# Seven Strassen pairs for the merge gates, with operand sums made from a stored modulated x

## The chip, the core and the metric

The kernel runs on one core of a Trainium2 chip. Its engines work from queues of their own and wait for each other by semaphores: TensorE (PE in the profile; its weight loads are shown as PEld), VectorE (DVE), ScalarE (ACT) and GpSimd (POOL). SyncE (SP) issues nearly all loads; POOL issues the stores that the code calls `store`. The metric is the device time of one execution in microseconds. Three runs of the kernel before took 1413.15, 1414.62 and 1421.28 us; the median is 1414.62 us.

## The reference

One layer over 1024 tokens of width 1024, in two halves. The change is in the first, the token mixer:

```
h     = rmsnorm(x, pre_mix_g) * (1 + sc1) + sh1      # sc1, sh1: per channel, from c @ ada_w
proj  = h @ w_in                                     # GLU input, q k v, and the gates
u     = silu(layernorm(conv31(glu(proj))))           # causal depthwise convolution, 512 channels
y_conv = u @ w_conv_out
y_att  = stick_breaking_attention(q, k, v) @ w_att_out
merged = sigmoid(g_conv) * y_conv + sigmoid(g_att) * y_att
y      = merged @ w_o
```

The gates `g_conv` and `g_att` are 2048 columns of `h @ w_in`, each a sum over the 1024 channels of h. After this half come its residual with a norm, and a SwiGLU block of the same manner. All is float32.

## The kernel before

**Data.** Channels lie on the partitions and tokens along the free axis. h is held as eight tiles of 128 channels by 1024 tokens, each as two parts, `hhi[k]` and `hlo[k]`, whose sum is h: a product of two such numbers is made by three matmuls (high x high, high x low, low x high) into a float32 bank of PSUM. A matmul takes 128x128 weights and streams 512 tokens. The 16 tiles of h live in the pool `hp`, tag `act`, which has 16 buffers.

**Start.** For each k, DVE multiplies x by the norm's factor and the scale (`x_op`, L310; the result stays in the tile `xs[k]`), ACT adds the shift and rounds (`hi_op`, L313), and DVE makes the low part (`lo_op`, L316).

**Attention stage.** Four heads' pairs are worked off with a raised priority; projections for the next pair, the GLU and the convolution (`conv`, L461) stand between them. The convolution's output goes to DRAM, `u_d`.

**Gates.** The 2048 gate columns are 16 blocks of 128, and two neighbouring blocks make a pair i = 0 to 7. A plain gate block (list `PLAIN`, L611 on; tile `pg`) takes 8 x 3 x 2 = 48 matmuls. A Strassen pair takes the 2x2 block product (two output blocks by two halves of the channels, times two halves of the channels by two halves of the tokens) in seven block products of 4 x 3 = 12 matmuls each instead of eight. `B11`, `B21` and `B22` are quarters of h itself, read from `hhi` and `hlo`; `T1` to `T4` are differences and sums of quarters, each held as a high and a low part for j = 0 to 3. `NPL = 2` makes pairs 6 and 7 plain and pairs 0 to 5 Strassen pairs.

The six Strassen pairs are made in two steps. The *early products* (loop over `GPAIRS`, the last in the attention stage's block; tiles `k1`, `k2`, `ee`) are the two that need no T: A11 B11, which goes to DRAM as `e_d0`, and A12 B21, which added to it gives the first gate quarter. Then, in a new scope with a new pool `pg` in the place of the attention's pools, DVE rebuilds h in `f` (L664, L665: `hhi + hlo`), makes four sums (L667 to L670) and ACT and DVE split them (`make_t`); `other_five(i)` makes the other five products for each pair and the gates' sigmoids, with `e_d0` loaded back as `p1`. Gates go to DRAM as `s_d`.

**LN and merge.** `ln_all` loads `u_d` into `cr` tiles and does the layer norm and silu of the convolution. It stands after pair 0 (`LN_AT = 0`) with a slightly raised priority, and its tiles come from `hp`, tag `act`. `y_conv` (tile `pyc`) multiplies it by `w_conv_out` and the gates, `y_att` (the loop that follows, tile `pya`) does it for the attention; then come the output projection (`pwo`) and the SwiGLU block (from L958 on).

**Order.** A planner orders each engine's instructions: it follows a model of the engines and takes at each point the ready instruction that stands first in the code, priorities aside. A tile needs a free buffer of its tag; the pools that matter here are `wp` (`wraw`, `whi` and `wlo`: three buffers each, for weights as loaded and for their parts), `hp`, and in `pg` the tags `f` (2), `x` (7), `s` (4) and `op` (16). PSUM banks are `psm` (3) and `psg` (4 and one for LN), dealt out by `bkg`. The order is fixed when the program is built; semaphores hold it on the chip.

Of the kernel before, what the change touches and what calls it, by code (L numbers as in the profile page):

```python
# [18 lines left out]
P = 128  # L19
D = 1024  # L20
T = 1024
KT = D // P
CH = 512
# [14 lines left out]
SH_DVE = (5, 6, 7)  # L38
NADA = 5
LATER = 100000  # L40
NPL = 2
GORDER = (0, 1, 2, 3, 4, 5, 6, 7)
NXT = 7
NWT = 4
# [31 lines left out]
def tile_block(ctx: ExitStack, tc: tile.TileContext, xT, vecs, ada1, ada2, win, wv, wcv, wat, wo, w1, w2, cvw, out):  # L76
    nc = tc.nc
    act, dve, pool, pe = nc.scalar, nc.vector, nc.gpsimd, nc.tensor
# [12 lines left out]
    u_d = [dp.tile([NG, P, TM], F32, name=f"u_d{k}") for k in range(CONVT)]  # L91
    cb_d = dp.tile([P, D], F32, name="cb_d")
    s_d = [dp.tile([P, T], F32, name=f"s_d{n}") for n in range(2 * KT)]
    e_d0 = [dp.tile([P, CH], F32, name=f"e_d0_{i}") for i in range(KT)]
    g_d = [dp.tile([P, 2, 2, CH], F32, name=f"g_d{k}") for k in range(FH)]
    w_d = [dp.tile([P, 4, 2, CH], F32, name=f"w_d{k}") for k in range(FH)]

# [5 lines left out]
    def load(dst, src):  # L103
        return nc.sync.dma_start(dst, src)

    def store(dst, src):
        nc.gpsimd.dma_start(dst, src)
# [19 lines left out]
    mod = small.tile([P, 48], F32, name="mod")  # L127
# [68 lines left out]
    hhi, hlo = [], []  # L196
# [6 lines left out]
    def bank(name):  # L203
        return psm.tile([P, CH], F32, tag="main", name=name)
# [5 lines left out]
    sgp = mkpool(sS, "sgp")  # L210
    with ExitStack() as s0:
# [7 lines left out]
        aws, xs, w0s, w0raw = {}, [], [], []  # L219
# [12 lines left out]
        with tc.high_priority(offset=3 * SOONER):  # L232
# [4 lines left out]
            for k in range(KT):  # L237
                load_ada(k)
                if k in W0_AT:
                    raw = wp.tile([P, T], F32, tag="wraw", name=f"w0raw{len(w0raw)}")  # L240
# [74 lines left out]
        def lo_op(k):  # L315
            dve.scalar_tensor_tensor(hlo[k], xs[k], shift_of(k), hhi[k], op0=ALU.add, op1=ALU.subtract)  # L316
# [41 lines left out]
        for k in range(KT):  # L358
            kn = k + 1
            if kn < KT:  # L360
                if kn not in SH_DVE:
                    shift_act(kn)
                if kn + 1 < KT and kn + 1 not in SH_DVE:
                    shift_pe(kn + 1)
                x_op(kn)
                if kn <= 2:
                    w0_hi(kn)
                hi_op(kn)
                if kn + 1 < KT:
                    dots(kn + 1)  # L370
                if kn <= 2:
                    w0_lo(kn)
            if k:
                lo_op(k)
            ws = (q0b, k0b, gg0b)
            if k <= 1:
                for i in range(k + 1):
                    gemm_k(ws[i], w0s[i], k)
                for kk in range(k + 1):
                    gemm_k(ws[k + 1], w0s[k + 1], kk)  # L380
            else:
                for b_, w_ in zip(ws, w0s):
                    gemm_k(b_, w_, k)
# [3 lines left out]
        for c in range(NCH):  # L387
            sg = sgp.tile([P, CH], F32, tag="sg", name=f"sg0_{c}", bufs=2)
# [4 lines left out]
    HK = KT // 2  # L393
    GP = dve
    GPAIRS = GORDER[:KT - NPL]
# [3 lines left out]
    def w_op(name, src, hi_eng, lo_eng):  # L399
        t = wp.tile([P, 2, CH], F32R, tag=("whi", "wlo")[next(uid) % 2], name=name)  # L400
        copy_to(hi_eng, t[:, 0], src)
        lo_eng.tensor_tensor(t[:, 1], src, t[:, 0], op=ALU.subtract)
        return t[:, 0], t[:, 1]

    def prod0(bank_, w, b, first=True):
        for j in range(HK):
            cols = slice(j * P, (j + 1) * P)
            if b[0] == "T":
                mvs = B0[b, j][:, 0], B0[b, j][:, 1]
            else:  # L410
                k = j + (HK if b in ("B21", "B22") else 0)
                cs = slice(CH, T) if b == "B22" else slice(0, CH)
                mvs = hhi[k][:, cs], hlo[k][:, cs]
            for s, (st, mv) in enumerate(((0, 0), (0, 1), (1, 0))):
                pe.matmul(bank_, w[st][:, cols], mvs[mv], start=(first and j == 0 and s == 0),
                          stop=(j == HK - 1 and s == 2), skip_group_check=not first)

    with ExitStack() as sC:
        pc = mkpool(sC, "pc")
        with ExitStack() as sA:  # L420
# [181 lines left out]
            v = v_half(0)  # L602
# [8 lines left out]
            for n in PLAIN:  # L611
                gb = banks2(f"pg{n}")
                gemm(gb, load_w(win[20 + n], f"wg{n}"), h, range(KT))
                for c in range(NCH):
                    sg = sgp.tile([P, CH], F32, tag="sg", name=f"sg{n}_{c}", bufs=2)
                    act.activation(sg, gb[c], AF.Sigmoid, bias=0.0, scale=1.0)
                    store(s_d[n][:, c * CH:(c + 1) * CH], sg)
            for i in GPAIRS:
                raw = wp.tile([P, T], F32, tag="wraw", name=f"ew{i}")
                load(raw, win[20 + 2 * i])  # L620
                e = [sgp.tile([P, CH], F32, tag="sg", name=f"ee{q}_{i}", bufs=2) for q in range(2)]
                k1 = bank(f"k1_{i}")
                prod0(k1, w_op(f"a11_{i}", raw[:, :CH], act, dve), "B11")
                act.activation(e[0], k1, AF.Copy)
                store(e_d0[i], e[0])
                k2 = bank(f"k2_{i}")
                prod0(k2, w_op(f"a12_{i}", raw[:, CH:], act, dve), "B21")
                dve.tensor_tensor(e[1], k2, e[0], op=ALU.add)
                act.activation(e[1], e[1], AF.Sigmoid, bias=0.0, scale=1.0)
                store(s_d[2 * i][:, :CH], e[1])  # L630

    sV.close()
    with ExitStack() as sG:
# [6 lines left out]
        def xt(name):  # L640
            return pg.tile([P, CH], F32, tag="x", name=name, bufs=NXT)
# [6 lines left out]
        def bkg(name):  # L648
            if next(uidg) % 7 in (1, 4, 6):
                return bank(name)  # L650
            return psg.tile([P, CH], F32, tag="m", name=name)
# [4 lines left out]
        def make_t(name, src, hi_eng, lo_eng):  # L656
# [2 lines left out]
            lo_eng.tensor_tensor(t[:, 1], src, t[:, 0], op=ALU.subtract)  # L659
            return t  # L660

        for j in range(HK):
            f = [pg.tile([P, T], F32, tag="f", name=f"f{q}_{j}", bufs=2) for q in range(2)]
            dve.tensor_tensor(f[0], hhi[j], hlo[j], op=ALU.add)  # L664
            dve.tensor_tensor(f[1], hhi[HK + j], hlo[HK + j], op=ALU.add)  # L665
            b11, b12, b21, b22 = f[0][:, :CH], f[0][:, CH:], f[1][:, :CH], f[1][:, CH:]
            dve.tensor_tensor(b11, b12, b11, op=ALU.subtract)  # L667
            dve.tensor_tensor(b12, b22, b12, op=ALU.subtract)
            dve.tensor_tensor(b22, b22, b11, op=ALU.subtract)
            dve.tensor_tensor(b21, b21, b22, op=ALU.subtract)  # L670
            for b, src in (("T2", b22), ("T3", b12), ("T1", b11), ("T4", b21)):
                B0[b, j] = make_t(f"{b}o_{j}", src, act, dve)

        pairs, p1s = {}, {}

        def pair_load(i):
            wg = wp.tile([P, T], F32, tag="wraw", name=f"gw{i}a")
            load(wg, win[20 + 2 * i])
            wu = wp.tile([P, T], F32, tag="wraw", name=f"gw{i}b")
            load(wu, win[21 + 2 * i])  # L680
            pairs[i] = wg, wu
            p1s[i] = xt(f"ga{i}")
            load(p1s[i], e_d0[i])

        def sig_out(t, n, c):
            act.activation(t, t, AF.Sigmoid, bias=0.0, scale=1.0)
            store(s_d[n][:, c * CH:(c + 1) * CH], t)

        def other_five(i):
            wg, wu = pairs[i]  # L690
            p1 = p1s[i]
            a11, a12, a21, a22 = wg[:, :CH], wg[:, CH:], wu[:, :CH], wu[:, CH:]
            s1, s2, s3 = (st(f"g{nm}_{i}") for nm in ("s1", "s2", "s3"))
            v, w_, c21 = xt(f"gv_{i}"), xt(f"gw_{i}"), xt(f"gc_{i}")
            dve.tensor_tensor(s1, a21, a22, op=ALU.add)
            dve.tensor_tensor(s2, s1, a11, op=ALU.subtract)
            s2o = w_op(f"s2o_{i}", s2, act, GP)
            dve.tensor_tensor(s3, a11, a21, op=ALU.subtract)
            s4 = s2
            dve.tensor_tensor(s4, a12, s2, op=ALU.subtract)  # L700
            ka, kc = bkg(f"ka_{i}"), bkg(f"kc_{i}")
            prod0(ka, s2o, "T2")
            dve.tensor_tensor(v, ka, p1, op=ALU.add)
            prod0(kc, w_op(f"s1o_{i}", s1, act, GP), "T1")
            dve.tensor_tensor(w_, kc, p1, op=ALU.add)
            prod0(ka, w_op(f"s3o_{i}", s3, act, GP), "T3", False)
            dve.tensor_tensor(w_, ka, w_, op=ALU.add)
            sig_out(w_, 2 * i + 1, 1)
            prod0(kc, w_op(f"s4o_{i}", s4, act, dve), "B22", False)
            dve.tensor_tensor(v, kc, v, op=ALU.add)  # L710
            sig_out(v, 2 * i, 1)
            prod0(ka, w_op(f"a22_{i}", a22, act, dve), "T4", False)
            dve.tensor_tensor(c21, ka, p1, op=ALU.add)
            sig_out(c21, 2 * i + 1, 0)

        cacc, chi, clo, yc, wcs = [], [], [], [], {}

# [70 lines left out]
        for q, i in enumerate(GPAIRS):  # L788
            if q + 1 < len(GPAIRS):
                pair_load(GPAIRS[q + 1])  # L790
            other_five(i)
            if q == LN_AT:
                with tc.high_priority(offset=LN_PRI):
                    ln_all()
# [55 lines left out]
    HK = KT // 2  # L850
# [940 lines left out]
```

## Time and profile before

| | us |
|---|---|
| median of three runs | 1414.62 |
| span of the profiled execution | 1415.0 (its time outside the span isn't shown) |
| PE busy | 1383.6 (98%) |
| DVE busy | 1060.4 (75%) |
| ACT busy | 651.3 (46%) |
| POOL busy | 96.7 (7%) |

The page gives one execution: busy time of each engine, the chain of work that ended last, and groups of like instructions with what ended the idle time before them. Matmuls overlap in PE's pipeline: one of 512 columns lasts 0.39 us in the rows but the next one begins 0.23 us after it, so counts per stretch tell more than busy shares. In the changed stage the plain gates run from 410 to 457 us, the early products to 492, pairs and LN to about 585, with y_conv from 570.7, y_att from 622.5 and the output projection from 666.

### The profile page before, as it was taken

How to read it: one execution, taken by the hardware profiler on the slowest of the kernel's cores; microseconds unless marked ns; L12 is line 12 of the kernel's file. 1: busy time of each engine (PE TensorE's matmuls, PEld its weight loads, DVE VectorE, ACT ScalarE, POOL GpSimd, SP SyncE). 2: the span in 40 equal slices, each digit the busy share in tenths (PEclk: the TensorE clock that was granted, in tenths of full speed). 3: DMA queues.
4: the chain of work that ended last, by engine and by line, in shares of the span. 5: the costliest groups of instructions: out<-in, count | busy, mean ns of one | idle time of the engine just before them, and what ended most of it. 6: DMA issues, size and time to landing. Idle time of an engine off the chain costs nothing.

```text
span 1415.0 us, 18809 instructions
## 1 busy us (share of the span) xinstructions
PE 1383.6 (98%) x6886; PEld 1156.1 (82%) x6886; DVE 1060.4 (75%) x1602; ACT 651.3 (46%) x1136; POOL 96.7 (7%) x183
## 2 busy tenths in 40 slices
PE   7999999999999999999999999999999999999996
PEld 4798898898888878888877778888888887888886
DVE  6898598576767789779588878778877775775357
ACT  5375465364553447412356553334444453334441
POOL 0000000000001110000012100001111110000000
PEclk8999999999999999999999999999999999999998
DMA  9112041131253645784935545456777769588833
GB/s 382 74 37 75 30 141 54 45 114 66 77 177 111 228 179 175 280 277 137 361 120 173 185 147 173 157 173 228 242 255 246 259 245 392 170 333 280 281 116 119
DMA packets 91116, 258.73 MB, mean 183 GB/s; under 512 B 9744, under 2 KB 20112, under 8 KB 90000
## 3 DMA queue, kind: packets, MB, share of 16 engines
q1 hardware_dynamic: 75088, 202.99, 42.1%
q0 software_dynamic: 15936, 54.54, 10.3%
q8 instruction: 54, 0.88, 0.3%
q14 instruction: 38, 0.31, 0.1%
HBM read 190.91 MB, written 66.58 MB: 182 GB/s over the span
## 4 chain that ended last, share of the span: by engine, by line
PE 80%; DVE 6%; issue 6%; DMA 5%; ACT 2%; POOL 1%; SPq 0%; DVEq 0%; POOLq 0%; ACTq 0%
PE ka L958 12%; PE ka L1500 8%; PE kc L958 7%; PE pwo L881 6%; PE pb L1500 4%; PE pgv L180 3%; PE pg L180 3%; PE pyc L180 3%; PE pya L180 3%; PE pv L481 3%; PE pcv L461 3%; PE tr L571 2%; PE pq L180 2%; PE pgg L180 2%; PE pk L180 2%
## 5 line engine op out<-in xcount | busy, mean ns | idle before, releaser
L559 DVE TENSOR_TENSOR_SCAN ka<-ka 128x128 f32<-128x128 f32 (+2 forms) x96 | 91.4, 968 | 22.8 <-ACT ka L555 22.5
L555 ACT ACTIVATE ka<-z 128x128 f32<-128x128 f32 (+2 forms) x96 | 47.1, 496 | 58.8 <-PE z L554 34.4
L575 DVE TENSOR_TENSOR alo<-tr,ahi 128x512 fp32r<-128x512 f32 x80 | 53.2, 685 | 18.2 <-ACT ahi L574 17.5
L1500 PE MATMUL ka<-gt,w2f 128*128 128x512 f32 x264 | 63.4, 390 | 0.8 <-DMA w2f<-w_d 0.8
L574 ACT ACTIVATE ahi<-tr 128x512 fp32r<-128x512 f32 x80 | 46.3, 601 | 38.1 <-PE tr L571 25.8
L561 DVE TENSOR_TENSOR be<-be,ka 128x127 f32<-128x127 f32 (+2 forms) x96 | 53.4, 573 | 9.6 <-ACT be L556 4.9
L1500 PEld LDWEIGHTS ka<-gt,w2f 128*128 128x128 f32 x264 | 49.4, 188 | 11.5 <-issue 1.4
L1066 PE MATMUL ke<-b,w_hi 128*128 128x512 f32 x176 | 55.2, 394 | 0.0
L135 DVE SCALAR_TENSOR_TENSOR ada<-ada,cb 128x1024 f32<-128x1024 f32 x32 | 38.8, 1223 | 20.7 <-DMA ada<-in_ada_dram 20.6
L556 ACT ACTIVATE be<-z 128x128 f32<-128x128 f32 (+2 forms) x96 | 46.2, 495 | 9.5 <-PE tr L571 9.3
L571 PE MATMUL tr<-ident,be 128*128 128x128 f32 x288 | 47.8, 273 | 0.4 <-DVE alo L575 0.4
L580 PE MATMUL av<-ahi,vst 128*128 128x256 f32 x160 | 44.2, 292 | 0.0
L461 PE MATMUL pcv<-ph,cvw 128*128 128x128 f32 x320 | 42.5, 276 | 0.8 <-DMA ph<-v_d 0.8
L581 PE MATMUL av<-alo,vst 128*128 128x256 f32 x160 | 42.8, 293 | 0.0
L461 PEld LDWEIGHTS pcv<-ph,cvw 128*128 128x128 f32 x320 | 39.5, 192 | 1.5 <-issue 1.2
L1066 PEld LDWEIGHTS ke<-b,w_hi 128*128 128x128 f32 x176 | 33.0, 188 | 7.8 <-issue 1.0
L481 PE MATMUL pv<-wv_hi,hhi 128*128 128x256 f32 x128 | 36.8, 288 | 2.1 <-DVE qst L505 1.4
L159 ACT ACTIVATE gt<-X 128x512 fp32r<-128x512 f32 x33 | 20.4, 630 | 39.5 <-DVE X L1543 12.4
L481 PE MATMUL pv<-wv_hi,hlo 128*128 128x256 f32 x128 | 36.7, 287 | 0.0
L481 PE MATMUL pv<-wv_lo,hhi 128*128 128x256 f32 x128 | 36.4, 285 | 0.0
L551 PE MATMUL z<-kst,qst 128*128 128x256 f32 (+2 forms) x96 | 36.2, 382 | 0.0
L571 PEld LDWEIGHTS tr<-ident,be 128*128 128x128 f32 x288 | 34.7, 140 | 1.8 <-PE z L554 0.5
(533 smaller groups left out, 4097.7 us busy)
## 6 DMA issues: line engine op xcount, KB each, us to landing
w_d<-w2o POOLq DMA_DIRECT2D x44, 512.0 KB, 8.0
w2f<-w_d SPq DMA_DIRECT2D x44, 512.0 KB, 5.4
ada<-in_ada_dram SPq DMA_DIRECT2D x32, 512.0 KB, 6.1
w2r<-in_w_dram SPq DMA_DIRECT2D x44, 256.0 KB, 3.8
w1g<-in_w_dram SPq DMA_DIRECT2D x21, 512.0 KB, 3.6
w1u<-in_w_dram SPq DMA_DIRECT2D x21, 512.0 KB, 5.2
cvw<-in_cvw_dram SPq DMA_DIRECT2D x20, 512.0 KB, 3.7
ada_w<-in_ada_dram SPq DMA_DIRECT2D x8, 1024.0 KB, 12.0
```

The costliest lines, as they stand in the source:

```text
L180: pe.matmul(bank, st[:, cols], mv[k][:, c * CH:(c + 1) * CH], start=(i == 0 and s == 0), stop=(i == n - 1 and s == 2))
L461: pe.matmul(cv[:, gi * TM:(gi + 1) * TM], wts[n][:, at:at + P], ph[:, g, SH - 1 - d:SH - 1 - d + TM], start=(d == 0), stop=(d == SH - 1))
L481: pe.matmul(pv[:, :256], st[k][:, tcols], mv[:, wc], start=(k == 0 and i == 0), stop=(k == KT - 1 and i == 2))
L555: act.activation(kap[:, s_lo:s_hi], z[:, zo:zo + w], AF.Sigmoid, bias=0.0, scale=-0.125)
L559: dve.tensor_tensor_scan(rev, rev, rev, init, op0=ALU.mult, op1=ALU.bypass)
L561: dve.tensor_tensor(beta[:, :m], beta[:, :m], kap[:, s_lo + 1:s_lo + 1 + m], op=ALU.mult)
L571: pe.transpose(tr[:, o:o + P], src, ident)
L575: dve.tensor_tensor(alo, tr, ahi, op=ALU.subtract)
L881: pe.matmul(bank_, st[:, cols], mv[k][:, cs], start=(k == 0 and q == 0), stop=(k == KT - 1 and q == 2))
L958: pe.matmul(bank_, st[:, cols], t[:, mv], start=(first and j == 0 and s == 0), stop=(j == HK - 1 and s == 2), skip_group_check=not first)
L1066: pe.matmul(kbs[f], wes[f][st][:, cols], t[:, mv], start=(i == 0 and j == 0 and q == 0), stop=(j == HK - 1 and q == 2), skip_group_check=i ...
L1500: pe.matmul(dst, w[st][:, cols], g[mv], start=first and s == 0, stop=last and s == 2, skip_group_check=more)
```

## The change

- `NPL = 1`: pair 6 becomes a Strassen pair, so there are seven of them and one plain pair.
- At the start each `xs[k]` (h without the shift) is stored to DRAM, `xm_d`, on POOL's queue. The quarters for the T sums are loaded from there instead of added up from `hhi` and `hlo`, for odd j into four `x` tiles, for even j into the two `f` tiles. The shift, the same for all tokens of a channel, cancels in T1; in T2, T3 and T4 it is added by the same DVE instruction (`scalar_tensor_tensor`, with `sh` or the difference `dsh1`).
- The early products and `e_d0` go. `strassen(i)` makes all seven products of a pair. Its T2 product is accumulated in the bank that holds A11 B11, after ACT has copied that out, and so are T3 and T4; `ka` so carries the running sum. ACT copies `v` and `w_` out where DVE added `p1` before. A pair uses three banks instead of two.

```diff
-NPL = 2
+NPL = 1
...
-    e_d0 = [dp.tile([P, CH], F32, name=f"e_d0_{i}") for i in range(KT)]
+    xm_d = [dp.tile([P, T], F32, name=f"xm_d{k}") for k in range(KT)]
...
             if k:
                 lo_op(k)
+            store(xm_d[k], xs[k])
...
-            for i in GPAIRS:
-                raw = wp.tile([P, T], F32, tag="wraw", name=f"ew{i}")
-                load(raw, win[20 + 2 * i])
-                e = [sgp.tile([P, CH], F32, tag="sg", name=f"ee{q}_{i}", bufs=2) for q in range(2)]
-                k1 = bank(f"k1_{i}")
-                prod0(k1, w_op(f"a11_{i}", raw[:, :CH], act, dve), "B11")
-                act.activation(e[0], k1, AF.Copy)
-                store(e_d0[i], e[0])
-                k2 = bank(f"k2_{i}")
-                prod0(k2, w_op(f"a12_{i}", raw[:, CH:], act, dve), "B21")
-                dve.tensor_tensor(e[1], k2, e[0], op=ALU.add)
-                act.activation(e[1], e[1], AF.Sigmoid, bias=0.0, scale=1.0)
-                store(s_d[2 * i][:, :CH], e[1])
...
+        dsh1 = small.tile([P, HK], F32, name="dsh1")
+        dve.tensor_tensor(dsh1, mod[:, HK:KT], mod[:, 0:HK], op=ALU.subtract)
         for j in range(HK):
-            f = [pg.tile([P, T], F32, tag="f", name=f"f{q}_{j}", bufs=2) for q in range(2)]
-            dve.tensor_tensor(f[0], hhi[j], hlo[j], op=ALU.add)
-            dve.tensor_tensor(f[1], hhi[HK + j], hlo[HK + j], op=ALU.add)
-            b11, b12, b21, b22 = f[0][:, :CH], f[0][:, CH:], f[1][:, :CH], f[1][:, CH:]
+            if j % 2:
+                b12, b11, b22, b21 = (xt(f"f{q}_{j}") for q in range(4))
+            else:
+                f = [pg.tile([P, T], F32, tag="f", name=f"f{q}_{j}", bufs=2) for q in range(2)]
+                b11, b12, b21, b22 = f[0][:, :CH], f[0][:, CH:], f[1][:, :CH], f[1][:, CH:]
+            for b, k, c in ((b12, j, 1), (b11, j, 0), (b22, HK + j, 1), (b21, HK + j, 0)):
+                load(b, xm_d[k][:, c * CH:(c + 1) * CH])
+            sh, ds = mod[:, HK + j:HK + j + 1], dsh1[:, j:j + 1]
             dve.tensor_tensor(b11, b12, b11, op=ALU.subtract)
-            dve.tensor_tensor(b12, b22, b12, op=ALU.subtract)
-            dve.tensor_tensor(b22, b22, b11, op=ALU.subtract)
-            dve.tensor_tensor(b21, b21, b22, op=ALU.subtract)
+            dve.scalar_tensor_tensor(b12, b22, ds, b12, op0=ALU.add, op1=ALU.subtract)
+            dve.scalar_tensor_tensor(b22, b22, sh, b11, op0=ALU.add, op1=ALU.subtract)
+            dve.scalar_tensor_tensor(b21, b21, sh, b22, op0=ALU.add, op1=ALU.subtract)
...
-        def other_five(i):
+        def strassen(i):
             wg, wu = pairs[i]
-            p1 = p1s[i]
...
+            p1, v, w_, c21 = (xt(f"g{nm}_{i}") for nm in ("p", "v", "w", "c"))
+            ka, kb, kc = bkg(f"ka_{i}"), bkg(f"kb_{i}"), bkg(f"kc_{i}")
+            prod0(ka, w_op(f"a11_{i}", a11, act, dve), "B11")
+            act.activation(p1, ka, AF.Copy)
+            prod0(kb, w_op(f"a12_{i}", a12, act, dve), "B21")
+            dve.tensor_tensor(p1, kb, p1, op=ALU.add)
+            sig_out(p1, p1, 2 * i, 0)
...
-            prod0(ka, s2o, "T2")
-            dve.tensor_tensor(v, ka, p1, op=ALU.add)
+            prod0(ka, s2o, "T2", False)
+            act.activation(v, ka, AF.Copy)
             prod0(kc, w_op(f"s1o_{i}", s1, act, GP), "T1")
-            dve.tensor_tensor(w_, kc, p1, op=ALU.add)
+            act.activation(w_, kc, AF.Copy)
             prod0(ka, w_op(f"s3o_{i}", s3, act, GP), "T3", False)
             dve.tensor_tensor(w_, ka, w_, op=ALU.add)
...
             prod0(ka, w_op(f"a22_{i}", a22, act, dve), "T4", False)
-            dve.tensor_tensor(c21, ka, p1, op=ALU.add)
-            sig_out(c21, 2 * i + 1, 0)
+            sig_out(c21, ka, 2 * i + 1, 0)
```

More of the change, by code (lines that the diff above doesn't have):

```diff
@@ L660, in make_t @@
             return t
+        dsh1 = small.tile([P, HK], F32, name="dsh1")
+        dve.tensor_tensor(dsh1, mod[:, HK:KT], mod[:, 0:HK], op=ALU.subtract)
         for j in range(HK):
-            f = [pg.tile([P, T], F32, tag="f", name=f"f{q}_{j}", bufs=2) for q in range(2)]
-            dve.tensor_tensor(f[0], hhi[j], hlo[j], op=ALU.add)
-            dve.tensor_tensor(f[1], hhi[HK + j], hlo[HK + j], op=ALU.add)
-            b11, b12, b21, b22 = f[0][:, :CH], f[0][:, CH:], f[1][:, :CH], f[1][:, CH:]
+            if j % 2:
[6 more added lines that the diff above has]
+            sh, ds = mod[:, HK + j:HK + j + 1], dsh1[:, j:j + 1]
             dve.tensor_tensor(b11, b12, b11, op=ALU.subtract)
-            dve.tensor_tensor(b12, b22, b12, op=ALU.subtract)
-            dve.tensor_tensor(b22, b22, b11, op=ALU.subtract)
-            dve.tensor_tensor(b21, b21, b22, op=ALU.subtract)
-            for b, src in (("T2", b22), ("T3", b12), ("T1", b11), ("T4", b21)):
+            dve.scalar_tensor_tensor(b12, b22, ds, b12, op0=ALU.add, op1=ALU.subtract)
+            dve.scalar_tensor_tensor(b22, b22, sh, b11, op0=ALU.add, op1=ALU.subtract)
+            dve.scalar_tensor_tensor(b21, b21, sh, b22, op0=ALU.add, op1=ALU.subtract)
+            for b, src in (("T2", b22), ("T1", b11), ("T3", b12), ("T4", b21)):
                 B0[b, j] = make_t(f"{b}o_{j}", src, act, dve)
-        pairs, p1s = {}, {}
+        pairs = {}
         def pair_load(i):
@@ L681, in pair_load, with sig_out @@
             pairs[i] = wg, wu
[L682 to L686, printed above, removed]
+        def sig_out(t, src, n, c):
+            act.activation(t, src, AF.Sigmoid, bias=0.0, scale=1.0)
             store(s_d[n][:, c * CH:(c + 1) * CH], t)
-        def other_five(i):
+        def strassen(i):
             wg, wu = pairs[i]
-            p1 = p1s[i]
             a11, a12, a21, a22 = wg[:, :CH], wg[:, CH:], wu[:, :CH], wu[:, CH:]
             s1, s2, s3 = (st(f"g{nm}_{i}") for nm in ("s1", "s2", "s3"))
-            v, w_, c21 = xt(f"gv_{i}"), xt(f"gw_{i}"), xt(f"gc_{i}")
+            p1, v, w_, c21 = (xt(f"g{nm}_{i}") for nm in ("p", "v", "w", "c"))
[5 more added lines that the diff above has]
+            sig_out(p1, p1, 2 * i, 0)
             dve.tensor_tensor(s1, a21, a22, op=ALU.add)
@@ L700, in other_five @@
             dve.tensor_tensor(s4, a12, s2, op=ALU.subtract)
-            ka, kc = bkg(f"ka_{i}"), bkg(f"kc_{i}")
-            prod0(ka, s2o, "T2")
-            dve.tensor_tensor(v, ka, p1, op=ALU.add)
+            prod0(ka, s2o, "T2", False)
+            act.activation(v, ka, AF.Copy)
             prod0(kc, w_op(f"s1o_{i}", s1, act, GP), "T1")
-            dve.tensor_tensor(w_, kc, p1, op=ALU.add)
+            act.activation(w_, kc, AF.Copy)
             prod0(ka, w_op(f"s3o_{i}", s3, act, GP), "T3", False)
             dve.tensor_tensor(w_, ka, w_, op=ALU.add)
-            sig_out(w_, 2 * i + 1, 1)
+            sig_out(w_, w_, 2 * i + 1, 1)
             prod0(kc, w_op(f"s4o_{i}", s4, act, dve), "B22", False)
             dve.tensor_tensor(v, kc, v, op=ALU.add)
-            sig_out(v, 2 * i, 1)
+            sig_out(v, v, 2 * i, 1)
             prod0(ka, w_op(f"a22_{i}", a22, act, dve), "T4", False)
-            dve.tensor_tensor(c21, ka, p1, op=ALU.add)
-            sig_out(c21, 2 * i + 1, 0)
+            sig_out(c21, ka, 2 * i + 1, 0)
         cacc, chi, clo, yc, wcs = [], [], [], [], {}
@@ L790, in tile_block @@
                 pair_load(GPAIRS[q + 1])
-            other_five(i)
+            strassen(i)
             if q == LN_AT:
```

## The prediction

> **What bounds the kernel now.** I read the page, then sums over stretches, then the chain of waits in order of time, then the groups and the timeline around the change. TensorE (PE) is busy for nearly the whole span, and the chain that ends last runs over it.
>
> ```profile
> span 1415.0 us, 18809 instructions
> PE 1383.6 (98%) x6886; PEld 1156.1 (82%) x6886; DVE 1060.4 (75%) x1602; ACT 651.3 (46%) x1136; POOL 96.7 (7%) x183
> PE 80%; DVE 6%; issue 6%; DMA 5%; ACT 2%; POOL 1%; SPq 0%; DVEq 0%; POOLq 0%; ACTq 0%
> ```
>
> Matmul durations overlap, so "busy" isn't pace. The pace is in the chain of waits (start, us, what): 116 matmuls in 26.33 us are 0.227 us each.
>
> ```profile
> 430.84 26.33 PE pg L180 x116
> ...
> 522.65 0.86 PE lnv L748 x2
> ...
> 570.73 6.46 PE pyc L180 x28
> ...
> 622.53 43.52 PE pya L180 x192
> ```
>
> Stretches of the stage that is changed (us; busy and count by engine; clock, DMA share, GB/s):
>
> ```profile
> core 0: us, PE busy (x) PEld busy (x) DVE busy (x) ACT busy (x) POOL busy (x), PEclk, DMA share, GB/s
> 410.00:457.00 47.00, 47.00 (x224) 39.36 (x222) 29.87 (x40) 17.63 (x34) 3.38 (x6) 1.00 0.39 128
> 457.00:492.00 35.00, 35.00 (x156) 29.01 (x155) 26.69 (x41) 18.30 (x35) 6.04 (x12) 1.00 0.63 206
> 492.00:515.00 23.00, 20.86 (x87) 15.49 (x86) 16.75 (x28) 9.63 (x18) 3.13 (x6) 1.00 0.61 225
> 515.00:570.00 55.00, 54.80 (x236) 43.88 (x235) 52.55 (x77) 38.08 (x52) 5.45 (x11) 1.00 0.52 177
> ```
>
> 410 to 457 is the plain gates, 457 to 492 the early products (with some of pair 0), then the Strassen pairs up to y_conv at 570.73. PE rests only 2.1 us in 492 to 515 and 0.2 us after. Each stage hides another engine's work: plain gates and early products hide the T operands, which DVE makes from 432 to 473; the pairs hide the LayerNorm of the convolution (LN below). So the question is what hides these two afterwards.
>
> **What it removes.** Pair 6 becomes a Strassen pair: 84 matmuls for 96, 12 x 0.227 = -2.7 us. Six early loads of weights, six stores and loads of e_d0 and eight DVE additions go; PE waited for none of them beyond the rests above. Per pair DVE keeps 14 operations and ACT goes from 8 to 14: at 0.69 us (the L746 row below) 9.7 us under 84 x 0.227 = 19.1 us of PE, so a pair by itself stays bound by PE. The rests go with LN's competition for DVE: -2.3 us. The new order within a pair (p1 and v copied out by ACT before PE accumulates on in ka) costs nothing: each copy has another bank's 12 matmuls, 2.7 us, over it; uncovered it would be 0.6 us (the 491.50 row below), twice a pair and 8 us over seven.
>
> **Stores at the start.** Eight stores of 512 KB follow the x products on POOL's queue, which holds nothing else there but a memset.
>
> ```profile
> L310 DVE SCALAR_TENSOR_TENSOR x<-x,scale,rstd x7: 1277/1280/1281, 29.4 to 57.2; 128x1024 f32<-128x1024 f32 x7
> ...
> L316 DVE SCALAR_TENSOR_TENSOR hlo<-x,mod,hhi x7: 1278/1279/1283, 36.9 to 59.7; 128x1024 fp32r<-128x1024 f32 x7
> L502 ACT ACTIVATE qst<-pq x4: 572/584/592, 67.0 to 143.5; 64x512 fp32r<-64x512 f32 x4
> w_d<-w2o POOLq DMA_DIRECT2D x44, 512.0 KB, 8.0
> ```
>
> The last product starts at 57.2 and takes 1.28 us; with 8.0 us to landing its store ends at 66.5. What takes over the buffers of that phase begins with qst at 67.0. I take 0; uncovered, it is the overhang of a store that lands late, 0 to 3 us.
>
> **T operands.** Now: the early products (first row) cover them until 492; f is first written right after the attention's last operation (oT), although its inputs, hhi and hlo, are there since 61 (the L316 row above): it waits for the attention's buffers, whose place the new pool takes.
>
> ```profile
> L415 PE MATMUL k<-hhi,a x96: 389/389/389, 457.0 to 492.1; 128*128 128x512 f32 x96
> ```
>
> ```profile
> 431.50 0.69 DVE L585 TENSOR_TENSOR oT<-av,oT 64x512 f32<-64x512 f32 x1 [5.66 <-ACT oT L584]
> 432.22 1.23 DVE L664 TENSOR_TENSOR f<-hhi,hlo 128x1024 f32<-128x1024 f32 x1
> ...
> 438.47 0.69 DVE L669 TENSOR_TENSOR f<-f,f 128x512 f32<-128x512 f32 x1
> 439.19 0.69 DVE L670 TENSOR_TENSOR f<-f 128x512 f32<-128x512 f32 x1
> 439.86 0.69 DVE L659 TENSOR_TENSOR T2o<-f,T2o 128x512 fp32r<-128x512 f32 x1
> ...
> 441.68 0.69 DVE L659 TENSOR_TENSOR T4o<-f,T4o 128x512 fp32r<-128x512 f32 x1
> 442.28 1.22 DVE L664 TENSOR_TENSOR f<-hhi,hlo 128x1024 f32<-128x1024 f32 x1
> ```
>
> ```profile
> ga<-e_d SPq DMA_DIRECT2D x6, 256.0 KB, 3.7
> ```
>
> After: loads of xm issue at 432.2 at the earliest; four of 256 KB, 3.7 us to landing, leave DVE starting about 436.5. Behind them on SP stand the loads of j = 2, which wait for f, and whatever is queued later; the weights of pair 0 can come before. Four sums at 0.7 and four low parts at 0.6 us (439.86 to 442.28) make 5.2 us for each j. The T2 of j = 3 follows three j, three sums, one ACT copy and one low part: 436.5 + 15.6 + 2.1 + 1.2 = 455.4. PE ends 96 plain gates at 457.0 - 96 x 0.227 = 435.2, and B11 and B21 of pair 0 (24) at 440.7. Until 455.4 it has T2 and T1 of j = 0 to 2 (18) and, as buffers allow, pair 1's B11 (12): 6.8 us. Idle: 14.7 - 6.8 = **+7.9 us**. Bounds: 0, if later pairs' products fill it; or DVE at its pace of now (10.1 us between 432.22 and the next j at 442.28), 436.5 + 30.3 + 3.3 = 470.1, idle 22.6. I take 7.9, because hardly anything else is left for DVE there.
>
> **LN.** In the code its tiles come from the pool hp: 16 buffers, all held by hhi and hlo. Those of j 0 to 3 come free when B11 has been multiplied for the last time. The trace agrees: the last store to u_d was issued at 413.50, but LN's loads (cr) went out at 490.69, when the sixth B11 was being finished (its copy to ee at 491.50).
>
> ```profile
> 413.50 0.38 SPq L104 DMA_DIRECT2D u_d<-co  x1
> ...
> 490.69 1.98 SPq L104 DMA_DIRECT2D cr<-u_d  x4
> ```
>
> ```profile
> 491.50 0.58 ACT L624 ACTIVATE ee<-k 128x512 f32<-128x512 f32 x1
> ```
>
> ```profile
> DMA to landing us min/median/max: 4.7/7.0/9.0
> ```
>
> ```profile
> L760 DVE TENSOR_TENSOR csil<-cr,csig 128x1024 f32<-128x1024 f32 x4 | 8.7, 2178 | 0.0
> L751 DVE TENSOR_TENSOR cr<-cr,la 128x512 f32<-128x512 f32 x8 | 5.0, 686 | 0.0
> L741 DVE TENSOR_TENSOR cr<-cr,lm 128x512 f32<-128x512 f32 x8 | 5.0, 684 | 0.0
> L721 DVE TENSOR_TENSOR clo<-csil,chi 128x1024 fp32r<-128x1024 f32 x4 | 4.9, 1227 | 0.0
> ...
> L746 DVE TENSOR_TENSOR la<-la,ls 128x512 f32<-128x512 f32 x6 | 4.1, 684 | 0.0
> ```
>
> After, the last B11 is the first product of the last pair, so LN starts seven products, not five pairs, before y_conv. DVE needs 8.7 + 5.0 + 5.0 + 4.9 + 4.1 for these rows and 12 more operations by the code (L734, L736, L153 to L155) at 0.684: 35.9 us, after a load of 7.0: 42.9 us. The buffers of j 0 and 1 are free after six matmuls, 1.4 us, and PE then has 19.1 - 1.4 = 17.7 us left: idle **+25.2 us**. (y_conv can begin on the first quarter a few us before the last low part; LN's waits on PE and ACT cost about as much. I leave both out.) The eight matmuls of LN (0.86 us for two, 3.4 in all) then stand in this gap: **-3.4 us**. Bounds: LN among all pairs took 570.73 - 490.69 = 80.0 us, which would leave 62.3; and y_att, 192 matmuls in 43.5 us which don't need LN, would fill it to 0 if they could go first. I take 25.2, by DVE's rows: only the last pair's eight or so DVE operations compete, and y_conv's weights, which come first in the code, fill the three buffers each of whi and wlo that y_att's would need.
>
> **Clock.** After the sparse PE work around 25 us the granted clock was half while full matmuls ran from 30.4 on.
>
> ```profile
> 30.00:32.00 2.00, 2.00 (x7) 0.50 1.00 418
> ...
> 34.00:36.00 2.00, 2.00 (x16) 0.89 1.03 416
> ```
>
> Some 4 us at half clock lose 2 us. Two new gaps: **+4 us**, between 0 (gaps broken up by single products) and 4. [...] No such gap amid full products is in this trace.
>
> **Sum.** Against the profiled span, 1415.0: -2.7 - 2.3 + 7.9 + 25.2 - 3.4 + 4.0 = 1443.7. The page gives no time around the span; the median of the runs, 1414.62, is 0.4 lower, so 1443.
>
> **Rivals.**
> *LN covered.* y_att goes ahead of y_conv and fills the gap. Without LN's 25.2, its -3.4 and one clock term: 1415.0 - 2.7 - 2.3 + 7.9 + 2.0 = 1419.9, 1419 or 1420. For it: it is ready work, and the planner does reorder: T2 of pair 0 began at 478.8, among the early products that ran until 492.
>
> ```profile
> L415 PE MATMUL ka<-T2o,s2o x72: 387/389/500, 478.8 to 567.6; 128*128 128x512 f32 x72
> ```
>
> Against it: the weight buffers. Chance 0.16.
>
> *Both covered, the other side.* Where the T operands are late, the planner brings B11 of later pairs forward, and B11 of the last pair early enough for LN to end before the last pair does: 1415.0 - 2.7 - 2.3 = 1410.0. It decides from the point where the last B11 ends 43 us (DVE alone) to 80 us (as now) before the pairs end, two to four pairs early. Against it: three buffers for the raw weights and three each for their parts let PE run about one pair ahead. Chance 0.08.
>
> *LN slowed.* It shares DVE and the in-order queues as now, 62.3 for 25.2: 1443 + 37 = 1480. Against it: one pair's DVE work is left beside it, where there were five. Chance 0.06.
>
> **Chances.** Forecast 0.70, with a range of its own of 1428 to 1462 (T idle from 0 to 15, LN's from 17 to 40). The predicted range reaches down to the LN-covered case and leaves out the two ends: 1417 to 1463. A measurement of this kernel tells about 0.5%, 7 us, from no change. Faster is the case with both covered, 0.08. LN covered lies at +0.4%, on the border: 0.06 of it, with T partly filled, counts as same and 0.10 as slower, with 0.70 and 0.06 from the others: 0.86.
>
> **What would show it.** cr's loads at about 435.2 + 7.9 + 6 x 19.1 + 1.4 = 559 instead of 490.69; a PE gap of about 25 us before the first y_conv product and one of 8 in T2 and T1 of pair 0; 12 matmuls fewer; half clock after both gaps. Wrong: cr loads before the last pair, or y_att's matmuls ahead of y_conv's.

## The result and the profile after

The changed kernel takes 1455.41 us (median of five runs, 1454.92 to 1460.54) beside 1415.1 us (median of five, 1413.15 to 1421.28) of the kernel before: a ratio of 1.029, with a 95% interval of 1.0272 to 1.0307. It is 40 us slower; 28 were forecast. Two executions below are left out of the ratios because they took far longer than the others of their kernel: 3596.39 us of the kernel before, and 2323.97 us of the one with no plain pairs.

The page of the kernel after, its span, its busy times and its chain of waits by engine:

```profile
span 1453.2 us, 18811 instructions
PE 1390.3 (96%) x6874; PEld 1158.9 (80%) x6874; DVE 1051.0 (72%) x1589; ACT 664.2 (46%) x1156; POOL 97.7 (7%) x185
PE 85%; DVE 6%; issue 4%; ACT 3%; DMA 1%; POOL 1%; SPq 0%; DVEq 0%; POOLq 0%; ACTq 0%
```

PE has 12 matmuls fewer, as the change says, and still the span is 38.2 us longer: PE's share fell from 98 to 96%. So the time went into waits of PE. The chain's shares by engine don't show which (PE even has more of it, 85% for 80); a table by stretches does. Stretches of the changed stage of the kernel after (us; busy and count by engine; clock, DMA share, GB/s):

```profile
core 0: us, PE busy (x) PEld busy (x) DVE busy (x) ACT busy (x) POOL busy (x), PEclk, DMA share, GB/s
410.90:435.40 24.50, 24.50 (x121) 20.66 (x121) 9.62 (x15) 8.00 (x18) 1.12 (x2) 1.00 0.39 128
435.40:465.00 29.60, 20.11 (x62) 13.92 (x61) 27.41 (x44) 14.69 (x27) 1.61 (x3) 0.83 0.60 209
465.00:588.00 123.00, 122.02 (x533) 99.69 (x532) 62.87 (x97) 56.68 (x96) 14.09 (x26) 1.00 0.48 162
588.00:617.30 29.30, 3.37 (x5) 0.80 (x4) 26.18 (x30) 24.72 (x27) 0.54 (x1) 0.60 0.58 202
617.30:662.90 45.60, 45.58 (x193) 37.62 (x194) 33.41 (x48) 6.45 (x7) 0.00 (x0) 0.96 0.52 171
662.90:706.40 43.50, 43.50 (x193) 36.02 (x192) 34.90 (x50) 11.28 (x12) 0.00 (x0) 1.00 0.40 130
```

And the same stage of the kernel before (pairs and LN; y_conv; y_att):

```profile
410.70:570.70 160.00, 157.66 (x693) 127.62 (x693) 126.57 (x187) 83.64 (x137) 18.52 (x34) 1.00 0.52 176
570.70:622.50 51.80, 51.80 (x230) 42.74 (x229) 37.62 (x51) 14.07 (x16) 2.17 (x4) 1.00 0.79 286
622.50:666.00 43.50, 43.50 (x194) 36.03 (x193) 38.50 (x59) 9.88 (x10) 0.00 (x0) 1.00 0.54 175
```

Count matmuls at 0.227 us each. The plain gates end at 435.4. In the next 29.6 us PE makes 62 matmuls, 14.1 us of work: **15.5 us are lost on the T operands**. Then 123 us of pairs run at full pace but for 2 us (533 matmuls, 121.0 us). Then **PE stands for 29.3 us with five matmuls, four of them LN's own**, until y_conv, while DVE is busy for 26.2 and ACT for 24.7. At last y_conv takes 45.6 us where y_att takes 43.5 for the same 192 matmuls. The stage grew from 255.3 us to 295.5. The rest of the program is 2.0 us shorter in this profiled execution. In ten of the eleven traces, the part from the output projection's first product to the end, which is the same code in all of them, takes from 746.8 to 749.2 us (749.1 in the kernel before, 747.0 in the kernel after); I have no cause for that.

### The profile page after: what moved, and what is told of

Same layout as the page of the kernel before. It is cut to its first block, busy times and chain, and to the rows that moved or that the text cites. A ratio compares the mean times of both kernels' runs of the same rounds, so it can differ in the third digit from the quotient of the medians.

```text
span 1453.2 us, 18811 instructions
## 1 busy us (share of the span) xinstructions
PE 1390.3 (96%) x6874; PEld 1158.9 (80%) x6874; DVE 1051.0 (72%) x1589; ACT 664.2 (46%) x1156; POOL 97.7 (7%) x185
## 4 chain that ended last, share of the span: by engine, by line
PE 85%; DVE 6%; issue 4%; ACT 3%; DMA 1%; POOL 1%; SPq 0%; DVEq 0%; POOLq 0%; ACTq 0%
PE ka L953 14%; PE ka L1495 8%; PE kc L953 8%; PE pwo L876 6%; PE ka L416 5%; PE pb L1495 4%; PE pyc L180 3%; PE pgv L180 3%; PE pya L180 3%; PE pv L482 3%; PE kc L416 3%; PE pcv L462 3%; PE tr L572 2%; PE pq L180 2%; PE pgg L180 2%
## 5 line engine op out<-in xcount | busy, mean ns | idle before, releaser
L159 ACT ACTIVATE gt<-X 128x512 fp32r<-128x512 f32 x33 | 20.4, 630 | 39.5 <-PE ka L1495 13.7
L159 ACT ACTIVATE s1o<-s 128x512 fp32r<-128x512 f32 x22 | 13.8, 629 | 49.8 <-PE ka L953 43.3
```

## The experiments

The theory was, of the two gaps: LN starts late because its buffers come free only with the last B11, and T is late because the plain gates no longer cover it. Each experiment below was timed against the kernel before on the same chip, where that took 1415.3 to 1415.7 us.

### One part alone: the last pair's early products held back

The kernel before keeps everything but the order: only the two early products of the last pair (pair 5, NPL = 2) move to the head of that pair.

```diff
-            for i in GPAIRS:
+            for i in GPAIRS[:-1]:
...
+            if i == GPAIRS[-1]:
+                e1, k1, k2 = xt(f"ge{i}"), bkg(f"k1_{i}"), bkg(f"k2_{i}")
+                prod0(k1, w_op(f"a11_{i}", a11, act, dve), "B11")
+                act.activation(p1, k1, AF.Copy)
+                prod0(k2, w_op(f"a12_{i}", a12, act, dve), "B21")
...
```

> The kernel before, with only the last pair's two early products (24 matmuls) moved to the head of that pair; the work is the same. My theory (LN's tiles wait for hhi and hlo of j 0 to 3, which the last B11 holds): cr's loads go from 490 to the last pair or a little ahead of it, y_conv waits for LN 20 to 30 us with PE idle at half clock, 1437 to 1447. Rival, that LN is late for another reason (its priority, its place after pair 0, the queues): cr's loads stay at 490 and the time within 3 us of before.

Measured: 1450.14 us, ratio 1.0232 (1.0205 to 1.0258). Twenty-four matmuls in another place cost 34.5 us. LN's loads, and the stretch ahead of y_conv:

```profile
L104 SPq DMA_DIRECT2D cr<-u_d x4: 326/352/487, 542.7 to 546.7; - x4
```

```profile
580.00:610.00 30.00, 2.07 (x2) 0.50 (x2) 22.59 (x25) 21.98 (x25) 1.08 (x2) 0.53 0.44 140
```

The loads go out 52 us later than before (490.69), and PE then makes two matmuls in 30 us. This is a part of the change alone with none of its new operations: the last reader of B11 sets when LN can start, and that alone is enough for the larger gap. The cost is 3 us over the range given, for the same reason as in the forecast (below): LN took 67 us from its loads to y_conv at 610.0, far more than DVE's rows add up to.

### What LN costs in each kernel

Both kernels without `ln_all`'s norm and silu: the convolution's output is loaded and goes into y_conv as it is, so the output differs, and the loads and their buffers stay. The diff is the same for both:

```diff
-            for c in range(NCH):
-                cs = slice(c * CH, (c + 1) * CH)
-                la, lm, ls = (hp.tile([P, 2, CH], F32, tag="act", name=f"l{nm}{c}") for nm in "ams")
...
-                cacc[ct] = o
```

Of the kernel after:

> The changed kernel without the layer norm and silu of the convolution: the raw convolution (cr, still in hp's buffers, still loaded when these come free) is split and multiplied, so the output is another. My theory: the gap ahead of y_conv is LN's own chain; loads (5 us) and the split (5 us) fit under the products that are left, so the gap of 29 us, its 2 us of half clock and LN's 3.4 us of matmuls go: 1419 to 1424. Rival, that y_conv waits for something else that comes late with the last pair (its weights, the gates from DRAM): 1440 or more.

Of the kernel before:

> The same left out of the kernel before, as the measure of what LN costs where it is hidden: 3.4 us of matmuls and the 2.3 us in which PE rested: 1409 to 1412. Were LN a cost there too, it would be 20 us or more.

Measured: after without LN 1422.74 us (ratio 1.0054, 1.0041 to 1.0068), before without LN 1410.31 us (0.9964, 0.995 to 0.9977), both inside their ranges. LN costs 1455.41 - 1422.74 = 32.7 us in the changed kernel and some 5.2 us in the kernel before, so **27.5 us of the 40 are LN coming out from under the pairs**, and 1422.74 - 1410.31 = 12.4 us are everything else. The trace of the changed kernel without LN shows that everything else is the T gap, and that the gap before y_conv is gone:

```profile
435.00:465.00 30.00, 19.61 (x66) 13.41 (x65) 27.47 (x44) 15.55 (x29) 1.61 (x3) 0.83 0.61 221
465.00:582.00 117.00, 116.31 (x513) 96.01 (x512) 57.46 (x85) 54.39 (x90) 12.96 (x24) 1.00 0.46 153
582.00:590.00 8.00, 8.00 (x37) 6.62 (x36) 2.05 (x3) 2.18 (x3) 1.62 (x3) 1.00 1.03 416
```

66 matmuls in the 30 us from 435 are 15.0 us of work, so 15.0 are lost; with the 12 matmuls saved, 2.7, that leaves 12.3 of the 12.4.

### Two plain pairs again in the changed kernel

```diff
-NPL = 1
+NPL = 2
```

> The changed kernel with pair 6 plain again (NPL = 2). My theory: 22 us of plain gates more cover the T operands, whose gap of 16 us goes, against 2.7 us for 12 matmuls; LN's gap of 29 us stays: 1440 to 1443. Rival, that the new order within a pair (ACT copies, sums kept in the bank) is what costs: one pair less of it, a seventh of 40 us, 1450.

Measured: 1443.27 us, ratio 1.0184 (1.0163 to 1.0205): 0.3 us above the range, and far from the rival's 1450, so the new order within a pair is not what costs. Stretches of it:

```profile
436.00:460.00 24.00, 24.00 (x108) 19.87 (x107) 22.60 (x36) 12.34 (x25) 3.21 (x6) 1.00 0.71 235
460.00:490.00 30.00, 30.00 (x134) 24.86 (x133) 18.01 (x29) 14.55 (x27) 2.69 (x5) 1.00 0.49 148
576.00:605.30 29.30, 2.98 (x4) 0.58 (x3) 25.34 (x29) 22.73 (x25) 0.54 (x1) 0.54 0.50 181
```

With a second plain pair, which makes 12 matmuls more in all, PE runs at full pace where the T gap was (242 matmuls, 54.9 us at pace, in the 54 us). The gap before y_conv stays as it was: 29.3 us with four matmuls. So the two gaps are separate. The T gap is worth 1455.41 - 1443.27 = 12.1 us and the 2.7 of those 12 matmuls: 14.9.

### T from hhi and hlo in the changed kernel

Is T late for the trip through DRAM, or for DVE's own work? Here `xm_d` goes and `f` is added up as before. (The order T2, T1, T3, T4 stays: the changed kernel splits T1 ahead of T3, the kernel before T3 ahead of T1.)

```diff
-            store(xm_d[k], xs[k])
...
-            for b, k, c in ((b12, j, 1), (b11, j, 0), (b22, HK + j, 1), (b21, HK + j, 0)):
-                load(b, xm_d[k][:, c * CH:(c + 1) * CH])
+            f = [pg.tile([P, T], F32, tag="f", name=f"f{q}_{j}", bufs=2) for q in range(2)]
+            dve.tensor_tensor(f[0], hhi[j], hlo[j], op=ALU.add)
+            dve.tensor_tensor(f[1], hhi[HK + j], hlo[HK + j], op=ALU.add)
...
```

> The changed kernel with the T operands summed from hhi and hlo again (no xm stores and loads). My theory: the T gap is set by DVE's queue. Eight additions of 1.2 us come back, 9.8 us, and the wait for the first loads of 5 us goes: 4 to 6 us slower than the changed kernel, 1459 to 1462. Rival, that the way through DRAM makes T late: 5 us faster or more, 1450 or less.

Measured: 1466.7 us, ratio 1.0349 (1.0327 to 1.0372): 11.3 us worse than the changed kernel, where 4 to 6 were expected. The last T2 low part and what PE waited for, in this kernel:

```profile
L646 DVE TENSOR_TENSOR T2o<-f,T2o x4: 685/691/692, 444.8 to 471.3; 128x512 fp32r<-128x512 f32 x4
```

```profile
L415 PE MATMUL ka<-T2o,s2o 128*128 128x512 f32 x12 | 7.3, 673 | 17.4 <-ACT T2o L159 15.3 <-DVE T2o L646 2.0
```

The last low part of T2 is made at 471.3, 8.6 us later than in the changed kernel (462.7), and PE stood 17.4 us ahead of T2 products. So the rival is out, and the trip through DRAM pays: it saves DVE eight additions of 1.23 us, 9.8 us. The 4 to 6 us were too few because I counted a gain of 5 us for the loads that needn't be waited for. There was none: the first low part of T2 starts at 444.8 here and at 444.4 in the changed kernel, where DVE works on pair 0's weights in half of that wait. It does stand there for 2.76 us until the first load lands (first row of its timeline below), so the trip isn't free; it costs less than the additions. Of the change's parts this one does what it is made for.

### Seven pairs alone

The kernel before with one plain pair; early products and T as they were.

```diff
-NPL = 2
+NPL = 1
```

> The kernel before with seven Strassen pairs alone (NPL = 1); early products, e_d0 and the sums from hhi and hlo stay. My theory (the loss comes from what no longer covers LN and the T operands, not from the seventh pair): 12 matmuls fewer, 2.7 us, with LN's loads 17 us earlier (22 us of plain gates less, 5 us of early products more), so 1412 against 1415, at most 1 us of T showing. Rival, that the plain gates of pair 6 were the cover which T needs: some 10 to 16 us slower, 1425 to 1431.

Measured: 1422.14 us, ratio 1.0042 (1.0029 to 1.0054): a miss by 10 us, slower for 12 matmuls fewer, and 3 us under the rival's range. The making of T2 in the kernel before and in this one (first and second row), and the stretch at the end of the early products:

```profile
L659 DVE TENSOR_TENSOR T2o<-f,T2o x4: 683/688/694, 439.9 to 469.9; 128x512 fp32r<-128x512 f32 x4
L659 DVE TENSOR_TENSOR T2o<-f,T2o x4: 677/682/685, 447.3 to 486.8; 128x512 fp32r<-128x512 f32 x4
```

```profile
439.20:479.50 40.30, 40.15 (x177) 32.87 (x176) 37.47 (x57) 22.44 (x41) 7.00 (x13) 1.00 0.62 206
479.50:500.00 20.50, 15.25 (x54) 10.53 (x54) 19.73 (x33) 9.09 (x17) 1.62 (x3) 0.92 0.64 223
```

I had held that early products cover T as well as plain gates do. They don't: they need DVE themselves (of the 37.5 us that it is busy in these 40.3, low parts of their weights take 6.9 and the additions to `ee` 4.1), so the last T2 came at 486.8 (469.9 before) and PE made 54 matmuls in the 20.5 us after the early products, losing 8.2. A plain gate needs DVE for its weights alone: one operation of 1.2 us in the first stretch of the table of after, where DVE is busy for 9.6 of 24.5 us, the most of it with the end of the attention and with pair 0. So the rival's mechanism is the one that held. In the profiled execution the plain gates also began at 414.4 instead of 410.4, after a slower first 80 us (300 matmuls made in them, 329 in the kernel before); the edit doesn't reach there, and I can't say why. (That execution took 1424.11 us, 2 more than the median.)

### xm with the early products kept: two, one and no plain pairs

Three kernels that are the one before with the stores and loads of `xm` and the new T sums, and nothing else of the change but NPL (2, 1, 0).

```diff
+            store(xm_d[k], xs[k])
...
-            dve.tensor_tensor(f[0], hhi[j], hlo[j], op=ALU.add)
+            for b, k, c in ((b12, j, 1), (b11, j, 0), (b22, HK + j, 1), (b21, HK + j, 0)):
+                load(b, xm_d[k][:, c * CH:(c + 1) * CH])
...
```

NPL = 1 and NPL = 0:

> The kernel before with seven pairs and its early products, T operands from xm in DRAM. With seven pairs alone the last T2 part came at 487, 8 us after the early products ended, and the loss was 6.5 us. My theory: DVE has 9.8 us less to do for the T operands and waits 3 to 5 us for the first loads, so the last T2 comes at 480 to 482 and hardly anything shows: 1412 to 1416. Rival, that the loads through DRAM are what holds: as slow as with the sums, 1420 to 1423, or slower.

> The same with all eight pairs as Strassen pairs: no plain gates, 16 early products (44 us) behind the attention. PE needs 5.4 us less than before; T's last part would come at about 480 against early products that end at 459 to 461: a gap of 15 us less what pair 0 and 1 can do: 1417 to 1427. If later pairs' work fills it, 1410.

Measured: 1420.99 us for one plain pair (ratio 1.0042, 1.0028 to 1.0056), a miss, inside the rival's range; and 1426.36 us for none (1.0079, 1.0063 to 1.0094), at the upper end of its range. PE's early products in the first and in the second:

```profile
L417 PE MATMUL k<-hhi,a 128*128 128x512 f32 x112 | 37.7, 407 | 5.3 <-DVE ee L630 4.0 <-ACT ee L626 1.4
```

```profile
L417 PE MATMUL k<-hhi,a 128*128 128x512 f32 x128 | 41.9, 402 | 3.6 <-DVE ee L630 3.6
```

With one plain pair, T was done 20 us sooner than with seven pairs alone (its last T2 at 466.8), so the loads are not what holds, although the time is the rival's. But now the early products themselves waited, 5.3 and 3.6 us, for the copies and additions to `ee` that hand their banks back: T's work and theirs stood in the same queues of DVE and ACT. The products of the pairs waited too, 3.6 us with one plain pair and 7.3 with none (2.4 in the kernel before). These rests are a part of the time above the forecast; I haven't added up the whole. That the time with none lies in its range is luck: the early products ended at about 465 and the last T2 came at 468.6, not at 480, so in place of the gap of 15 us that the range rests on there is one of some 4. That prompted the last run, two plain pairs:

> The kernel before with one part of the change alone: the eight stores of the x products at the start, and the T operands made from loads of them instead of hhi + hlo; two plain gates, six pairs with early products, four-operation order of T as before. My theory (the stores cost nothing, and T is covered by the plain gates and early products whichever way it is made): 1413 to 1417 us, with f's first operation some 5 us later than before (about 437) and the T operands done 20 us earlier. The rival that the two misses with early products suggest (the faster T takes DVE and ACT from the copies out of the early products, and PE waits for ee): 1418 to 1424 us, with PE rests in the early products that end on ee.

Measured: 1418.24 us, ratio 1.0018 (1.0007 to 1.0029). The early products, and the last T2:

```profile
L417 PE MATMUL k<-hhi,a 128*128 128x512 f32 x96 | 30.3, 392 | 0.4 <-DVE ee L630 0.4
```

```profile
437.70 0.69 DVE L675 TENSOR_TENSOR f<-f 128x512 f32<-128x512 f32 x1
...
458.09 0.68 DVE L661 TENSOR_TENSOR T2o<-f,T2o 128x512 fp32r<-128x512 f32 x1
```

PE waited 0.4 us for `ee`, so the rival's mechanism is out where two plain pairs run ahead; and yet the time lies in the rival's range, 1.0 to 4.1 us above the kernel before by the interval and just over mine. T was done 12 us sooner (20 were expected) under work that hid it anyway, and the kernel gained nothing by it. Where the few us go is not shown: the profiled execution, 1416.15 us, is the shortest of the twelve, and in it the output projection begins 1.2 us later than in the kernel before. With the early products kept, none of the three was faster than the kernel before.

## Why the prediction was right, and where it was short

The sign, the two places and the order of the sizes came out; the likeliest case occurred, 12 us above its number though inside its own range. Step by step:

**12 matmuls, the stores, the rests.** 6874 matmuls for 6886: -2.7 as said. The plain gates begin at 410.9, as before within 0.5 us, so the eight stores at the start cost nothing there, as said. The rests of the pairs didn't all go: 2.0 us of 123, of which LN's four matmuls that still fell among the products take 0.8 more than their pace. That is -1.1 for -2.3.

**T operands: the term that was mis-sized.** Forecast 7.9 and 2.0 for the clock, measured 15.5 in all. The step that failed is "hardly anything else is left for DVE there". DVE's timeline in the kernel after (start, duration, what):

```profile
437.12 0.69 DVE L661 TENSOR_TENSOR f<-f 128x512 f32<-128x512 f32 x1 [2.76 <-DMA f<-xm_d]
437.73 0.68 DVE L403 TENSOR_TENSOR s2o<-gs,s2o 128x512 fp32r<-128x512 f32 x1
...
443.22 0.69 DVE L403 TENSOR_TENSOR s4o<-gs,s4o 128x512 fp32r<-128x512 f32 x1
443.82 0.69 DVE L403 TENSOR_TENSOR a<-gw1a,a 128x512 fp32r<-128x512 f32 x1
...
462.67 0.69 DVE L647 TENSOR_TENSOR T2o<-f,T2o 128x512 fp32r<-128x512 f32 x1
```

The first sum starts at 437.12, forecast 436.5. The fourth T2 is done at 462.67 + 0.6 = 463.3, forecast 455.4: 7.9 late, 0.6 from the start and 7.3 from twelve operations of 0.6 us that stand in between (rows 2 to 4 are three of them): sums and low parts of the weights of pairs 0 and 1, which the seven products together need at once, and the addition of the first gate quarter. Forecast idle 7.9 and these 7.9 make 15.8, and 15.5 were lost, the slower clock included. What PE found to do meanwhile was as forecast, the 12 matmuls of pair 1's B11 among it. The run with two plain pairs and `xm` shows the same T work with only two operations in it that aren't T's: 437.70 to 458.09, 20.4 us for 25.6. PE's waits in the gap (idle before, and what ended it, in brackets); where it is ACT's high part, ACT had itself stood for a sum of DVE (4.83 us before the T2 part that it starts at 448.88):

```profile
443.05 0.50 PE L416 MATMUL kc<-T1o,s1o 128*128 128x512 f32 x1 [1.78 <-ACT T1o L159]
...
453.84 1.22 PE L416 MATMUL kc<-T1o,s1o 128*128 128x512 f32 x2 [3.25 <-DVE T1o L647]
...
460.28 0.51 PE L416 MATMUL ka<-T2o,s2o 128*128 128x512 f32 x1 [2.77 <-ACT T2o L159]
```

**LN: place right, size 4 us short, by two errors that nearly cancel.** LN's tiles in the kernel after, by operation (count: shortest, median, longest ns; first and last start):

```profile
L104 SPq DMA_DIRECT2D cr<-u_d x4: 327/426/430, 558.7 to 560.0; - x4
L751 ACT ACTIVATE csig<-cr,vec x4: 1225/1226/1240, 606.6 to 613.8; 128x1024 f32<-128x1024 f32 x4
```

```profile
L733 PE MATMUL lnm<-la,ones x4: 590/592/697, 570.9 to 589.1; 128*128 128x512 f32 x4
```

```profile
588.57 1.12 PE L733 MATMUL lnm<-la,ones 128*128 128x512 f32 x2 [0.40 <-ACT lm L152]
```

The loads went out at 558.7, forecast 559, but partly by luck. The T gap pushed them 8 us later than I had it, and the planner put the last pair's B11 into the pair ahead of it, right after that pair's T2, which brought them forward by the three products that came after it, 36 x 0.227 = 8.2 us. By the prediction's own words, loads of cr before the last pair were a sign of being wrong; they came in this form, and the gap was there all the same. From the loads to the end of the pairs it was 29.5 us, not 17.7: these three products and, for the other 3.6, mostly LN's own four matmuls and short rests among the products. On the other side LN took 58.7 us from the loads to y_conv, not 42.9. DVE alone doesn't set it: the prediction took the waits of LN on PE and ACT to be paid for by y_conv's early start and left both out, and that is the step that failed here. While products run, LN's matmuls wait in PE's queue behind them: the row of `la` that the first lnm needs starts at 566.6 and the matmul at 570.9.

```profile
L731 DVE TENSOR_TENSOR la<-la,cr x2: 685/688/692, 565.6 to 566.6; 128x512 f32<-128x512 f32 x2
```

In the gap DVE is busy for 26.2 of 29.3 us, but 6.1 of that is not LN's: the low parts of y_att's operands (`olo`) and one of y_conv's weights. Two groups of DVE in the stretch from 588 to 617.3, and the two that PE waits for (575 to 620):

```profile
L802 DVE TENSOR_TENSOR olo<-of,ohi 128x1024 fp32r<-128x1024 f32 x4 | 4.9, 1221 | 0.1
L169 DVE TENSOR_TENSOR wc_lo<-wc_raw,wc_hi 128x1024 fp32r<-128x1024 f32 x1 | 1.2, 1218 | 0.0
```

```profile
L743 PE MATMUL lnv<-la,ones 128*128 128x512 f32 x4 | 3.1, 866 | 10.0 <-DVE la L741 10.0
L180 PE MATMUL pyc<-chi,wc_hi 128*128 128x512 f32 x6 | 2.9, 656 | 15.6 <-ACT chi L159 15.6
```

The two halves of the tokens also run one after the other: LN has one PSUM bank, and the second half's sums were in `la` at 579.3 but its lnm began at 588.57, when ACT had read the first half's lnv out of the bank (`lm`). In PE's last 15.6 us of waiting, the end of the second half's norm takes the first 5, and then come the silu's eight activations of 1.24 us on ACT in a row, from 606.6 to 616.3, and the split. Gap: 58.7 - 29.5 = 29.2 (forecast 25.2). Of the -3.4 for LN's matmuls half came true, as four of the eight still ran among the products: -1.7.

**Clock.** The first gap, broken up by single products, had a mean clock of 0.83; what that cost beyond the wait for DVE isn't shown apart. After the second the clock was half while y_conv's first products ran:

```profile
595.00:600.00 5.00, 0.35 (x1) 0.35 (x2) 4.72 (x8) 3.27 (x6) 0.00 (x0) 0.50 0.87 256
618.00:620.00 2.00, 2.00 (x6) 1.57 (x5) 2.00 (x3) 2.00 (x3) 0.00 (x0) 0.50 0.00 0
620.00:622.00 2.00, 2.00 (x8) 1.59 (x7) 2.00 (x3) 0.11 (x1) 0.00 (x0) 0.73 0.00 0
622.00:624.00 2.00, 2.00 (x11) 1.65 (x10) 0.86 (x1) 0.00 (x0) 0.00 (x0) 1.00 0.00 0
```

From 617.3 it stays at half until about 621; in the chain y_conv's 192 matmuls last 45.54 us and y_att's 43.52:

```profile
617.32 45.54 PE pyc L180 x192
662.87 43.52 PE pya L180 x192
```

That is 2.0 us, the forecast's price of one gap; for the first gap no such price is shown apart.

**The rivals.** y_att didn't go first: its products start at 662.9, after y_conv's, so the case with LN covered did not occur. B11 of the last pair did come forward, the mechanism of the case with both covered, but 29.5 us before the pairs' end where LN turned out to need 58.7.

**Sum.** Measured: -2.7 - 1.1 + 15.5 + 29.3 - 1.7 + 2.0 = 41.3, for a stage that grew by 40.2 (forecast 28.7); 1.1 us are counted too much somewhere. The profiled execution of before that the forecast was summed against lay above the median too: a run lasts 1.7 us longer than its span (1454.92 for 1453.2), so 1415.0 belongs to a time of about 1416.7, where I took 1414.6. Those 2 us are most of why 40.3 us by medians are 38.2 by the spans.

## What to carry to other kernels

Ask of a step that is moved later not only what it computes but whose buffers its last read gives back: here two products in another place delayed an unrelated stage by 52 us and cost 34 us, with PE's work unchanged. Cover is worth only as much as the engine it leaves free: plain products hid DVE's work, products that need DVE for their own operands hid less of it. And a stage that was hidden can be longer than the sum of one engine's rows once it stands alone, as LN was here: its engines take turns, its halves share a bank, and it shares their queues with what comes next.

## What the runs showed that I had not expected

- LN, uncovered, ran 58.7 us from loads to y_conv while its busiest engine had 35.9 us of it by my count: 1.6 times the sum of its rows.
- Making T sooner hardly helped where the early products were kept. With one plain pair the ratio to the kernel before is 1.0042 with it and without it, and PE then waited 5.3 us for the copies and additions that hand PSUM banks back; with two, T had been hidden already. With none, there is no run without it to compare.
- In the 29 us gap the granted clock was 1.00 until 593 and 0.50 from 594, some 4 us after the LN matmuls at its start had ended (589.7). It was still 0.50 when y_conv's products began at 617.3, and 1.00 again from 621.5, some 4 us later. In the gap with single products its mean was 0.83.
